# Gated DeltaNet in a hybrid encoder trunk: decays read back as running sums, row groups taken in turn, products with the zero state left out

## The chip, the cores and the metric

The kernel runs on one core of a Trainium2 chip. The metric is the device time of one execution in microseconds (us). A core has TensorE (PE; its weight loads are listed apart as PEld), VectorE (DVE), ScalarE (ACT), GpSimd (POOL) and SyncE (SP), whose queue issues all DMA transfers of this kernel. Each engine works through its own instructions in the order in which they were written into its queue; semaphores hold an instruction back until what it reads is there and what it overwrites has been read. Two memories matter: SBUF, 128 partitions wide, and PSUM, into which TensorE writes.

## What is computed

One layer with three token mixers over 2048 positions, each on its own columns of one input projection:

```python
h = rmsnorm(x, norm_w[l])
u = jnp.einsum('bsd,de->bse', h, w_in[l])
(a_q, a_k, a_v, a_z, g_q, g_k, g_v, g_z, g_b, g_a, r_x, r_z) = jnp.split(u, SPLIT_POINTS, axis=-1)
y_a = diff_attention(a_q, a_k, a_v, ...) * jax.nn.silu(a_z)
y_g = gated_deltanet(g_q, g_k, g_v, g_b, g_a, g_z, ...)
y_r = rg_lru(r_x, ...) * jax.nn.silu(r_z)
x = x + jnp.einsum('bse,ed->bsd', concat(y_a, y_g, y_r), w_out[l])
return rmsnorm(x, final_norm_w)
```

The change is in the second mixer, the gated delta rule (GDN), with 4 heads of 128 columns. Its core, in chunks:

```python
g = jnp.cumsum(g, axis=-1)                     # log decay, summed inside a chunk
decay = jnp.exp(jnp.where(tri, g[..., :, None] - g[..., None, :], -jnp.inf))
Lmat = jnp.where(strict, einsum('id,jd->ij', k_beta, k) * decay, 0.0)
T = triangular_solve(eye + Lmat, eye, lower=True, unit_diagonal=True)
u = T @ v_beta;   w = T @ (k_beta * jnp.exp(g)[..., None])
a_intra = jnp.where(tri, einsum('id,jd->ij', q, k) * decay, 0.0)

def step(state, xs):                           # over the chunks; the first state is zero
    v_new = u_i - w_i @ state
    o = (q_i * exp(g_i)) @ state + a_i @ v_new
    state = state * exp(g_last) + (k_i * exp(g_last - g_i)).T @ v_new
    return state, o
```

## The kernel before

Positions are taken in two halves of 1024 (`hf`), each half in two blocks of 512 (`sb`). The first stage, up to about 1140 us, runs the input projections: a job is 128 columns of `w_in`, and `unit` (L294) makes 128 x 512 outputs of it in 24 products, three for each of 8 slices of the inner dimension, since every f32 operand is split into a high and a low part (L298 to L300). Results go to one of two PSUM buffers `pj`. Everything else of this stage runs as Python generators in `bgs`: after every second slice `unit` calls `pump`, which lets each generator write its next few instructions. So the work of the mixers is laid in small pieces between the projections. The tile framework's scheduler then fixes the order on each engine; the order of the program is its preference, and it moves instructions that would wait. The second stage runs attention and the output projection, and the change does not touch it but for the number of buffers of one tile (`sd`).

The delta rule uses chunks of 128 positions, eight to a half (`NC_H`). In each half `gb_post` (L386) makes the gates once for all heads: `g`, its split in `ghi` and `glo`, and by two small products the running sums and totals, whose exponentials are `gam` and `gl`. For each of four heads, `Gdn.main` (L489) then does the following.

1. Decays, for two groups of four chunks (L517 to L535). With `tri_le` the triangle of ones, GpSimd multiplies it by the chunk's `ghi` and by its `glo` (L522), 8 instructions a group. TensorE multiplies a strict triangle `tri_gt` with both (L528, L531), which gives all differences of running sums in one PSUM tile, and ScalarE takes the exponential into `dec` (L535).
2. Gram products of keys with keys and queries, 4 a group (L543), scaled by `dec` on VectorE (L549) into `la`; the 32x32 diagonal blocks go to DRAM (`ls`, L563) and come back in another layout (`lt`, L573).
3. The inverse. VectorE solves the 32x32 blocks (L590, L596); they pass through DRAM (`ts`) into `pi`, and are transposed into `xi` (L613). Then the blocks are joined on TensorE: a 32-row stage (L626, L635, L639, each product on one 32-row group of the array, for 8 chunks and two pairs of blocks) and a 64-row stage (L650, L658). The products on f32 data run as two passes each, so L626 is 16 products and 32 passes a head.
4. The chunks in turn (L671 to L706): L674 is the key product with the state, L683 the inverse applied to its difference to the values, L685 the query product with the state, L692 the update of the state, L693 the product inside the chunk. ScalarE evacuates twice (L689, L698), and VectorE does the rest.

SP issues the transfers of all this in one order, together with the fetches of weights (`wx`, L117), which run two jobs ahead.

## Time and profile before

| what | value |
|---|---|
| timed runs | 1777.53, 1775.45, 1775.56 us (median 1775.56) |
| profiled execution | 1779.44 us, span 1777.7 us |
| busy share of the span | PE 97%, PEld 81%, DVE 73%, ACT 56%, POOL 20% |
| granted TensorE clock, mean | 0.995 |

A busy share counts the time in which an engine had at least one instruction in work. Products overlap in TensorE, so a share near 100% alone does not say how much work there is: that is read from the starts of successive products. Lines of the profile are those of the kernel before; x2 behind a small product counts its passes. What an engine waited for is inferred from semaphores. Nothing of the second stage is read below, except that both stages share the same TensorE.

### The profile page before, as it was taken

How to read it: one execution, taken by the hardware profiler on the slowest of the kernel's cores; microseconds unless marked ns; L12 is line 12 of the kernel's file. 1: busy time of each engine (PE TensorE's matmuls, PEld its weight loads, DVE VectorE, ACT ScalarE, POOL GpSimd, SP SyncE). 2: the span in 40 equal slices, each digit the busy share in tenths (PEclk: the TensorE clock that was granted, in tenths of full speed). 3: DMA queues.
4: the chain of work that ended last, by engine and by line, in shares of the span. 5: the costliest groups of instructions: out<-in, count | busy, mean ns of one | idle time of the engine just before them, and what ended most of it. 6: DMA issues, size and time to landing. Idle time of an engine off the chain costs nothing.

```text
span 1777.7 us, 28350 instructions
## 1 busy us (share of the span) xinstructions
PE 1721.5 (97%) x9674; PEld 1433.7 (81%) x9674; DVE 1304.3 (73%) x3064; ACT 987.4 (56%) x2500; POOL 363.3 (20%) x591
## 2 busy tenths in 40 slices
PE   7999999999999999999999999989999999999998
PEld 6877878888878887787787888877888888887786
DVE  6566786686776566688678668568777877778896
ACT  6524534435434553352552543458878878877685
POOL 3211401301301122151151140011213213221011
PEclk9999999999999999999999999999999999999999
DMA  6123142241244423424535424597797797596442
GB/s 186 49 80 90 52 117 73 75 109 58 86 125 137 143 72 119 134 87 160 153 100 166 137 86 123 169 259 217 194 244 220 257 247 213 166 277 212 159 143 101
DMA packets 306901, 257.45 MB, mean 145 GB/s; under 512 B 66794, under 2 KB 242116, under 8 KB 306756
## 3 DMA queue, kind: packets, MB, share of 16 engines
q1 hardware_dynamic: 306756, 255.64, 49.6%
q8 instruction: 76, 1.25, 0.3%
q14 instruction: 69, 0.57, 0.1%
HBM read 171.69 MB, written 83.89 MB: 144 GB/s over the span
## 4 chain that ended last, share of the span: by engine, by line
PE 48%; DVE 11%; issue 5%; DMA 4%; POOL 3%; ACT 3%; SPq 0%; DVEq 0%; POOLq 0%; ACTq 0%
PE pj L298 6%; PE pj L299 6%; PE pj L300 6%; PE pj L885 4%; PE pj L883 4%; PE pj L884 4%; PE s L1026 3%; PE s L1027 2%; PE pt L1101 2%; DVE tt L596 1%; PE av L1119 1%; DVE tt L590 1%; PE av L1120 1%; DVE s L363 1%; PE av L1118 1%
## 5 line engine op out<-in xcount | busy, mean ns | idle before, releaser
L298 PE MATMUL pj<-hp,wx 128*128 128x512 f32 x1120 | 463.6, 414 | 2.7 <-DVE sz L375 1.2
L300 PE MATMUL pj<-hp,wx 128*128 128x512 f32 x1120 | 444.3, 397 | 0.0
L299 PE MATMUL pj<-hp,wx 128*128 128x512 f32 x1120 | 443.0, 396 | 0.0
L300 PEld LDWEIGHTS pj<-hp,wx 128*128 128x128 f32 x1120 | 210.6, 188 | 49.4
L298 PEld LDWEIGHTS pj<-hp,wx 128*128 128x128 f32 x1120 | 211.3, 189 | 45.3 <-DVE sz L375 1.4
L299 PEld LDWEIGHTS pj<-hp,wx 128*128 128x128 f32 x1120 | 211.8, 189 | 41.9
L1030 DVE TENSOR_REDUCE nm<-s 128x1 f32<-128x512 f32 (+3 forms) x320 | 191.7, 605 | 27.4 <-PE s L1027 24.0
L1038 ACT ACTIVATE s<-s,nm 128x512 f32<-128x512 f32 (+3 forms) x272 | 170.6, 629 | 52.6 <-DVE nm L1030 51.2
L363 DVE SCALAR_TENSOR_TENSOR s<-raw,pcol,s 128x512 f32<-128x512 f32 x192 | 144.5, 753 | 37.0 <-POOL s L359 34.5
L1026 PE MATMUL s<-hp 128*128 128x512 f32 (+3 forms) x320 | 124.5, 390 | 6.3 <-DMA hp<-k_sp 3.6
L291 DVE TENSOR_TENSOR wx<-wx 128x1024 fp32r<-128x1024 f32 (+1 forms) x77 | 95.6, 1242 | 44.3 <-ACT wx L287 44.2
L287 ACT ACTIVATE wx<-wx 128x1024 fp32r<-128x1024 f32 (+1 forms) x76 | 80.4, 1058 | 77.7 <-PE pj L299 67.2
L1027 PE MATMUL s<-hp 128*128 128x512 f32 (+3 forms) x320 | 117.8, 368 | 0.0
L1101 PE MATMUL pt<-ident,s 128*128 128x128 f32 x544 | 86.1, 274 | 4.0 <-DVE s L1089 3.9
L354 POOL COPY halo<-raw 128x3 f32<-128x3 f32 x48 | 13.2, 275 | 373.1 <-ACT raw L352 367.2
L883 PE MATMUL pj<-g,wx 128*128 128x512 f32 x208 | 85.4, 411 | 0.1
L590 DVE TENSOR_TENSOR tt<-lt,tt 128x248 f32<-128x248 f32 (+30 forms) x248 | 80.8, 326 | 6.5
L1089 DVE SCALAR_TENSOR_TENSOR s<-s,cf,s 128x512 f32<-128x512 f32 (+2 forms) x112 | 75.1, 702 | 11.1 <-ACT s L1077 6.5
L596 DVE TENSOR_TENSOR tt<-tt 128x248 f32<-128x248 f32 (+30 forms) x248 | 78.2, 315 | 6.4
L885 PE MATMUL pj<-g,wx 128*128 128x512 f32 x208 | 82.3, 396 | 0.0
L884 PE MATMUL pj<-g,wx 128*128 128x512 f32 x208 | 81.9, 394 | 0.0
L317 PE MATMUL pj<-wx,hp 128*128 128x264 f32 (+1 forms) x256 | 76.7, 301 | 2.9 <-ACT wx L287 0.9
(341 smaller groups left out, 3958.1 us busy)
## 6 DMA issues: line engine op xcount, KB each, us to landing
wx<-in_w_in_dram SPq DMA_DIRECT2D x78, 512.0 KB, 4.4
wx<-y_sp SPq DMA_DIRECT2D x64, 512.0 KB, 5.8
hp<-k_sp SPq DMA_DIRECT2D x64, 256.0 KB, 6.2
wo_sp<-s SPq DMA_DIRECT2D x48, 256.0 KB, 2.0
v_sp<-s SPq DMA_DIRECT2D x64, 128.0 KB, 2.9
q_sp<-s SPq DMA_DIRECT2D x32, 256.0 KB, 3.2
k_sp<-s SPq DMA_DIRECT2D x32, 256.0 KB, 2.6
y_sp<-go SPq DMA_DIRECT2D x32, 256.0 KB, 2.1
```

Source lines behind the costliest of these rows:

```text
L298: nc.tensor.matmul(ps, wh[:, kt, :], hb[kt][:, 0, :], start=(kt == 0), stop=False)
L299: nc.tensor.matmul(ps, wh[:, kt, :], hb[kt][:, 1, :], start=False, stop=False)
L300: nc.tensor.matmul(ps, wl[:, kt, :], hb[kt][:, 0, :], start=False, stop=(kt == KT - 1))
L363: nc.vector.scalar_tensor_tensor(y, raw[:, t : t + SB], pc(wcol(t)), y, op0=ALU.mult, op1=ALU.add)
L883: nc.tensor.matmul(ps, yh, wh, start=first, stop=False)
L884: nc.tensor.matmul(ps, yh, wl, start=False, stop=False)
L885: nc.tensor.matmul(ps, yl, wh, start=False, stop=last)
L1026: nc.tensor.matmul(ps[:, :n], qq, kh[:, :n], start=True, stop=False)
L1027: nc.tensor.matmul(ps[:, :n], qq, kl[:, :n], start=False, stop=True)
L1030: nc.vector.tensor_reduce(nm[:, u, m, kb : kb + 1], ps[:, :n], axis=AX.X, op=ALU.max, negate=True)
L1038: nc.scalar.activation(ee[:, :n], ps[:, :n], AF.Exp, bias=nm[:, u, m, kb : kb + 1], accum_out=zp[:, u, m, kb : kb + 1],)
L1101: nc.tensor.transpose(pt[:, off + (u - us[0]) * P : off + (u - us[0] + 1) * P], e[(u, kt // 4)][:, (kt % 4) * P : (kt % 4 + 1) * P], ident,)
```

## The change

It has four parts, all in the delta rule.

- Decays. `tri_gt`, `ghi` and `glo`, their GpSimd products and the two TensorE products a group go. Instead `gb_post` makes a third small product, the running sums with chunks in rows, writes them to DRAM (`cs`), and keeps the sums by position in `cum`. Each group reads its four rows of `cs` back, broadcast to all 128 partitions (256 KB in SBUF). ScalarE then takes ReLU(`cum` - value) by chunk, and the exponential of the negative. The reads and the exponentials stand at the start of `main`, before the wait for the keys, and `sd` has two buffers instead of one.
- Row groups. The products of the first two steps of the 32-row stage loop over chunks outside and pairs inside, so successive products are on different row groups.
- The transposed block. The third product of this stage (L639) and its VectorE operation become a 32x32 transpose of the second's result.
- State. For the first chunk of the first half the products with the zero state are left out, and the state is copied instead of updated; for the last chunk of the second half the update is left out.

```diff
@@ -148,12 +148,6 @@
     nc.gpsimd.affine_select(
         tri_le, ones32, pattern=[[1, P]], compare_op=ALU.is_ge, fill=0.0, base=0, channel_multiplier=-1
     )
-    tri_gt = ctile([P, P], "tri_gt", F32R)
-    tri_gt32 = at([P, P], "s16", 16)
-    nc.gpsimd.affine_select(
-        tri_gt32, ones32, pattern=[[-1, P]], compare_op=ALU.is_gt, fill=0.0, base=0, channel_multiplier=1
-    )
-    nc.vector.tensor_copy(tri_gt, tri_gt32)
 
     pcol = ctile([P, N_COLS], "pcol")
     nps = psum.tile([P, SB], F32, name="pps", tag="tp", bufs=3)
...
@@ -401,10 +393,6 @@
         g = at([P, 4, NC_H], "g", 2)
         nc.vector.scalar_tensor_tensor(g, xa, 0.0, ax, op0=ALU.max, op1=ALU.add)
         nc.vector.tensor_tensor(g, g, nea.unsqueeze(2).to_broadcast([P, 4, NC_H]), op=ALU.mult)
-        ghi = at([P, 4, NC_H], "ghi", 2, F32R)
-        nc.vector.tensor_copy(ghi, g)
-        glo = at([P, 4, NC_H], "glo", 2, F32R)
-        nc.vector.tensor_tensor(glo, g, ghi.bitcast(F32), op=ALU.subtract)
         yield
         yield
         yield
@@ -412,13 +400,21 @@
         gf = g.rearrange("p a b -> p (a b)")
         nc.tensor.matmul(pg[:, 0:32], tri_le, gf, start=True, stop=True)
         nc.tensor.matmul(pg[:, 32:64], ones, gf, start=True, stop=True)
+        nc.tensor.matmul(pg[0:32, 64 : 64 + P], gf, tri_le, start=True, stop=True)
...
+
+        cum = at([P, 4, NC_H], "cum", 1)
+        nc.scalar.activation(cum, pg[:, 0:32].rearrange("p (b c) -> p b c", b=4), AF.Copy)
+        cr = at([32, P], "s16", 16)
+        nc.scalar.activation(cr, pg[0:32, 64 : 64 + P], AF.Copy)
+        cs = dram.tile([4 * NC_H, P], F32, name="cs", tag="cs", bufs=2)
+        nc.sync.dma_start(cs, cr)
         ngam = at([P, 4, NC_H], "ngam", 2)
         nc.vector.tensor_scalar_mul(ngam, gam[:, 0], -1.0)
-        r.beta, r.ghi, r.glo, r.gam, r.gl, r.ngam = beta, ghi, glo, gam[:, 0], gam[:, 1], ngam
+        r.beta, r.cum, r.cs, r.gam, r.gl, r.ngam = beta, cum, cs, gam[:, 0], gam[:, 1], ngam
         r.ready = True
 
 
@@ -488,7 +484,26 @@
 
         def main(v):
             h, gbs = v.h, v.gbs
-            while v.nt < 4 or not gbs.ready:
+            while not gbs.ready:
+                yield
+            decs = [at([P, 4, P], "sd", 2) for _ in range(2)]
+            for sb in range(2):
+                r0 = h * NC_H + sb * 4
+                nc.sync.dma_start(
+                    decs[sb].rearrange("p c e -> p (c e)"),
+                    gbs.cs[r0 : r0 + 4].rearrange("r e -> (r e)").unsqueeze(0).to_broadcast([P, SB]),
+                )
+            yield from wait(4)
+            for sb in range(2):
+                for c in range(4):
+                    ci = sb * 4 + c
+                    nc.scalar.activation(
+                        decs[sb][:, c, :], decs[sb][:, c, :], AF.Relu, scale=-1.0,
+                        bias=gbs.cum[:, h, ci : ci + 1],
+                    )
+                nc.scalar.activation(decs[sb], decs[sb], AF.Exp, scale=-1.0)
+                yield
+            while v.nt < 4:
                 yield
             ss = v.ss
             nc.vector.tensor_scalar_add(ss, ss, 4e-6)
@@ -514,25 +529,9 @@
                 kq = v.kq[sb]
                 la = at([P, 4, 2, P], "g5", 5)
                 las.append(la)
-                gmh = at([P, 4, P], "s16", 16, F32R)
-                gml = at([P, 4, P], "s16", 16, F32R)
-                for c in range(4):
-                    ci = sb * 4 + c
-                    for gm, gg in ((gmh, gbs.ghi), (gml, gbs.glo)):
-                        nc.gpsimd.tensor_scalar(
-                            gm[:, c, :], tri_le, gg.bitcast(F32)[:, h, ci : ci + 1], 0.0,
-                            op0=ALU.mult, op1=ALU.add,
-                        )
+
+                dec = decs[sb]
                 yield from wait(3)
-                pe = tp()
-                nc.tensor.matmul(
-                    pe, tri_gt, gmh.rearrange("p c e -> p (c e)"), start=True, stop=False
-                )
-                nc.tensor.matmul(
-                    pe, tri_gt, gml.rearrange("p c e -> p (c e)"), start=False, stop=True
-                )
-                dec = at([P, 4, P], "sd", 1)
-                nc.scalar.activation(dec, pe.rearrange("p (c e) -> p c e", c=4), AF.Exp)
                 nc.vector.tensor_tensor(
                     cd[:, sb * 4 : sb * 4 + 4], cc[:, sb * 4 : sb * 4 + 4], dec[:, :, P - 1],
                     op=ALU.mult,
@@ -621,8 +620,8 @@
             ]
             zs32 = at([P, NC_H, 32], "zs", 1)
             pz = tp().rearrange("p (c e) -> p c e", c=NC_H)
-            for a, b in pairs:
-                for c in range(NC_H):
+            for c in range(NC_H):
+                for a, b in pairs:
                     nc.tensor.matmul(
                         pz[b, c, 0:32], lt_ab(c, a, b), xi[a, c, a], start=True, stop=True
                     )
@@ -630,19 +629,15 @@
                 nc.vector.tensor_copy(zs32[b], pz[b, :, 0:32])
             yield
             pu = tp().rearrange("p (c e) -> p c e", c=NC_H)
-            for a, b in pairs:
-                for c in range(NC_H):
+            for c in range(NC_H):
+                for a, b in pairs:
                     nc.tensor.matmul(
                         pu[a, c, 0:32], zs32[b, c, :], pi[b, c, b], start=True, stop=True
                     )
-            for c in range(NC_H):
-                nc.tensor.matmul(
-                    pu[32:64, c, 0:32], pi[32:64, c, 32:64], zs32[32:64, c, :],
-                    start=True, stop=True,
-                )
-            nc.vector.tensor_scalar_mul(xi[32:64, :, 0:32], pu[32:64, :, 0:32], -1.0)
             for a, b in pairs:
                 nc.vector.tensor_scalar_mul(pi[a, :, b], pu[a, :, 0:32], -1.0)
+
+            nc.vector.transpose(xi[32:64, :, 0:32], pi[0:32, :, 32:64])
             yield
             lo, up = slice(0, 64), slice(64, 128)
             pz = tp().rearrange("p (c e) -> p c e", c=NC_H)
@@ -670,36 +665,51 @@
                 so = at([P, 4], "so", 2)
                 for c in range(4):
                     ci = sb * 4 + c
-                    pks = psum.tile([P, P], F32, name="ch", tag="ch", bufs=2)
-                    nc.tensor.matmul(pks, v.kq[sb][:, c, 0, :], S_, start=True, stop=True)
+
+                    none, final = v.hf == 0 and ci == 0, v.hf == 1 and ci == NC_H - 1
                     ct = at([P, 4, P], "ct", 2)
-                    br = ct[:, 0, :]
-                    nc.vector.scalar_tensor_tensor(
-                        br, pks, gbs.ngam[:, h, ci : ci + 1], v.vb[sb][:, c, :],
-                        op0=ALU.mult, op1=ALU.add,
-                    )
-                    yield
+                    br = v.vb[sb][:, c, :]
+                    if not none:
...
+                        yield
                     py = psum.tile([P, P], F32, name="ch", tag="ch", bufs=2)
                     nc.tensor.matmul(py, pi[:, ci, :], br, start=True, stop=True)
                     po = psum.tile([P, 2, P], F32, name="oq", tag="oq", bufs=1)
-                    nc.tensor.matmul(po[:, 0, :], v.kq[sb][:, c, 1, :], S_, start=True, stop=True)
-                    yd = ct[:, 1, :]
-                    nc.vector.tensor_scalar(yd, py, cd[:, ci : ci + 1], None, op0=ALU.mult)
+                    if not none:
+                        nc.tensor.matmul(
+                            po[:, 0, :], v.kq[sb][:, c, 1, :], S_, start=True, stop=True
+                        )
+                    if not final:
+                        yd = ct[:, 1, :]
+                        nc.vector.tensor_scalar(yd, py, cd[:, ci : ci + 1], None, op0=ALU.mult)
                     y = ct[:, 2, :]
                     nc.scalar.activation(y, py, AF.Copy)
                     yield
-                    pst = psum.tile([P, P], F32, name="ch", tag="ch", bufs=2)
-                    nc.tensor.matmul(pst, v.kp[sb][:, c, :], yd, start=True, stop=True)
+                    if not final:
+                        pst = psum.tile([P, P], F32, name="ch", tag="ch", bufs=2)
+                        nc.tensor.matmul(pst, v.kp[sb][:, c, :], yd, start=True, stop=True)
                     nc.tensor.matmul(po[:, 1, :], las[sb][:, c, 1, :], y, start=True, stop=True)
-                    nc.vector.scalar_tensor_tensor(
-                        S_, S_, gbs.gl[:, h, ci : ci + 1], pst, op0=ALU.mult, op1=ALU.add
-                    )
-                    ay = ct[:, 3, :]
-                    nc.scalar.activation(ay, po[:, 1, :], AF.Copy)
-                    nc.vector.scalar_tensor_tensor(
-                        os_[:, c, :], po[:, 0, :], gbs.gam[:, h, ci : ci + 1], ay,
-                        op0=ALU.mult, op1=ALU.add,
-                    )
+                    if none:
+                        nc.vector.tensor_copy(S_, pst)
+                    elif not final:
+                        nc.vector.scalar_tensor_tensor(
+                            S_, S_, gbs.gl[:, h, ci : ci + 1], pst, op0=ALU.mult, op1=ALU.add
+                        )
+                    if none:
+                        nc.scalar.activation(os_[:, c, :], po[:, 1, :], AF.Copy)
+                    else:
+                        ay = ct[:, 3, :]
+                        nc.scalar.activation(ay, po[:, 1, :], AF.Copy)
+                        nc.vector.scalar_tensor_tensor(
+                            os_[:, c, :], po[:, 0, :], gbs.gam[:, h, ci : ci + 1], ay,
+                            op0=ALU.mult, op1=ALU.add,
+                        )
                     jk = at([P, SB], "junk", 1, BF16)
                     nc.scalar.activation(
                         jk[:, :P], os_[:, c, :], AF.Square, accum_out=so[:, c : c + 1]
@@ -913,7 +923,7 @@
-                pe = at([P, SB], "sd", 1)
+                pe = at([P, SB], "sd", 2)
```

Three places of the order on an engine follow, of the kernel before and of the changed one. Lines of the changed kernel are its own: L290 to L292 are the projection there (L298 to L300 before).

TensorE, first head, first group of decays, before (`s_1013` and `s_1014` are the two operands made by GpSimd):

```order
405 L298 MATMUL pj<-hp,wx 128x512
406 L299 MATMUL pj<-hp,wx 128x512
407 L300 MATMUL pj<-hp,wx 128x512
408 L528 MATMUL tp<-s_1013,tri_gt 128x512 [waits PE_49,Pool_49]
409 L531 MATMUL tp<-s_1014,tri_gt 128x512 [waits Pool_49]
410 L543 MATMUL tp<-g_608 128x256 x2
411 L543 MATMUL tp<-g_608 128x256 [waits Activation_49]
412 L543 MATMUL tp<-g_608 128x256
413 L298 MATMUL pj<-hp,wx 128x512
```

The same place in the changed kernel, where L542 is the Gram product:

```order
406 L290 MATMUL pj<-hp,wx 128x512
407 L291 MATMUL pj<-hp,wx 128x512
408 L292 MATMUL pj<-hp,wx 128x512
409 L542 MATMUL tp<-g_600 128x256 [waits PE_49]
410 L542 MATMUL tp<-g_600 128x256 x3
411 L290 MATMUL pj<-hp,wx 128x512
```

The two triangle products and their waits for GpSimd are gone; the Gram products follow the projection.

ScalarE, second head of the first half, second group, before (L477 evacuates the transposed values, L689 and L698 belong to the chunks of the head before):

```order
184 L371 ACTIVATE s_2245<-pj 128x512 [waits PE_49]
185 L535 ACTIVATE sd<-tp 128x512 [waits DVE_49,PE_49,Activation_49]
186 L689 ACTIVATE ct<-ch 128x128 [waits DVE_49]
187 L698 ACTIVATE ct<-oq 128x128 [waits PE_49]
188 L704 ACTIVATE junk,so<-go 128x128 [waits DVE_49]
189 L477 ACTIVATE s_2321<-tp,nk 128x128 [waits PE_49]
190 L477 ACTIVATE s_2321<-tp,nk 128x128 x3
```

The same place in the changed kernel (L500 is the ReLU, L504 the exponential):

```order
195 L363 ACTIVATE s_2206<-pj 128x512 [waits DMAHW1_49,PE_49]
196 L692 ACTIVATE ct<-ch 128x128 [waits DVE_49]
197 L708 ACTIVATE ct<-oq 128x128 [waits PE_49]
198 L714 ACTIVATE junk,so<-go 128x128 [waits DVE_49]
199 L500 ACTIVATE sd<-sd,cum 128x128 [waits DMAHW5_49]
200 L500 ACTIVATE sd<-sd,cum 128x128 x3
201 L504 ACTIVATE sd<-sd 128x512 [waits Activation_49]
202 L473 ACTIVATE s_2290<-tp,nk 128x128 [waits PE_49]
203 L473 ACTIVATE s_2290<-tp,nk 128x128 x3
204 L279 ACTIVATE wx<-wx 128x1024 [waits DMAHW6_49,PE_49]
205 L363 ACTIVATE s_2302<-pj 128x512 [waits DMAHW3_49,PE_49]
```

The exponential of a PSUM tile is replaced by four ReLUs and an exponential that wait for a transfer (DMAHW5), for the decays of the head after; they stand behind the chunk's evacuations and ahead of the transposed values.

SP at the same head in the changed kernel (before, the same eight writes L563 and then L573 stand without anything between):

```order
98 L562 DMA ls<-g_2081 32x4x32 [waits DMAHW1_49,DVE_49]
99 L562 DMA ls<-g_2081 32x4x32
100 L562 DMA ls<-g_2081 32x4x32 [waits DMAHW3_49]
101 L562 DMA ls<-g_2081 32x4x32
102 L492 DMA sd<-cs 128x512
103 L562 DMA ls<-g_2170 32x4x32 [waits DMAHW6_49,DVE_49]
104 L562 DMA ls<-g_2170 32x4x32 [waits DMAHW7_49]
105 L562 DMA ls<-g_2170 32x4x32 [waits DMAHW0_49]
106 L562 DMA ls<-g_2170 32x4x32 [waits DMAHW1_49]
107 L492 DMA sd<-cs 128x512 [waits DMAHW2_49]
108 L572 DMA lt<-ls 32x1024 [waits DMAHW4_49,DMAHW6_49,DMAHW3_49,DMAHW7_49,DMAHW1_49,DMAHW0_49]
```

Each broadcast read (L492) of the next head stands right behind the writes that follow the last use of the buffer it fills.

## Rows read from the trace of the kernel before

**Rows 1.** The page's busy times, and its chain of waits by line.
```profile
PE 1721.5 (97%) x9674; PEld 1433.7 (81%) x9674; DVE 1304.3 (73%) x3064; ACT 987.4 (56%) x2500; POOL 363.3 (20%) x591
...
PE pj L298 6%; PE pj L299 6%; PE pj L300 6%; PE pj L885 4%; PE pj L883 4%; PE pj L884 4%; PE s L1026 3%; PE s L1027 2%; PE pt L1101 2%; DVE tt L596 1%; PE av L1119 1%; DVE tt L590 1%; PE av L1120 1%; DVE s L363 1%; PE av L1118 1%
```

**Rows 2.** TensorE timeline near 306 us: start, length, line, operands, passes.
```profile
305.32 0.49 PE L683 MATMUL ch<-ct,g 128*128 128x128 f32 x2
...
306.10 0.40 PE L299 MATMUL pj<-hp,wx 128*128 128x512 f32 x1
306.33 0.39 PE L300 MATMUL pj<-hp,wx 128*128 128x512 f32 x1
...
307.24 0.38 PE L692 MATMUL ch<-ct,s 128*128 128x128 f32 x2
307.46 0.48 PE L693 MATMUL oq<-ct,g 128*128 128x128 f32 x2
307.70 0.48 PE L298 MATMUL pj<-hp,wx 128*128 128x512 f32 x1
308.02 0.40 PE L299 MATMUL pj<-hp,wx 128*128 128x512 f32 x1
```

**Rows 3.** Stretches: length, busy PE, PEld, DVE, ACT, POOL, then granted clock, DMA.
```profile
140.00:1140.00 1000.00, 981.59 (x5512) 805.00 (x5511) 718.96 (x1662) 435.55 (x1036) 211.43 (x383) 1.00 0.38 110
```

**Rows 4.** Waits of TensorE: total us, times, longest.
```profile
PE tp L528 <- POOL s L522: 2.7, 4, 1.3
```

**Rows 5.** Line L528 alone, idle before it with weight loads: us, times.
```profile
  POOL s L522: 7.5, 9
```

**Rows 6.** TensorE timeline, 32-row stage of the first head.
```profile
152.57 1.09 PE L626 MATMUL tp<-xi,g 32*32 32x32 f32 x32
153.60 0.50 PE L298 MATMUL pj<-hp,wx 128*128 128x512 f32 x1
...
156.01 0.21 PE L639 MATMUL tp<-zs,g 32*32 32x32 f32 x1
...
156.10 0.19 PE L635 MATMUL tp<-g,zs 32*32 32x32 f32 x1
156.12 0.57 PE L639 MATMUL tp<-zs,g 32*32 32x32 f32 x13
156.62 0.50 PE L298 MATMUL pj<-hp,wx 128*128 128x512 f32 x1
```

**Rows 7.** Groups by line: count, busy us, mean ns, idle before and its releaser.
```profile
L645 DVE TENSOR_SCALAR g<-tp 32x256 f32<-32x256 f32 x16 | 6.7, 417 | 0.5
...
L613 DVE STREAM_TRANSPOSE xi<-g 32x256 f32<-32x256 f32 x24 | 10.4, 433 | 13.2 <-DMA g<-ts 12.7
...
L371 ACT ACTIVATE s<-s 128x512 f32<-128x512 f32 x48 | 30.3, 631 | 63.4 <-DVE s L363 63.1
...
L689 ACT ACTIVATE ct<-ch 128x128 f32<-128x128 f32 x64 | 17.6, 275 | 66.1 <-DVE ct L687 66.1
```

**Rows 8.** ScalarE timeline, second head.
```profile
214.34 0.19 ACT L704 ACTIVATION_READ_ACCUMULATOR junk<-go 128x1 f32 x1
217.10 1.14 ACT L477 ACTIVATE s<-tp,nk 128x128 f32<-128x128 f32 x4 [2.57 <-PE tp L473]
...
219.21 0.58 ACT L371 ACTIVATE s<-pj 128x512 f32<-128x512 f32 x1
```

**Rows 9.** SP timeline, second head.
```profile
211.29 5.33 SPq L563 DMA_DIRECT2D ls<-g  x8
```

**Rows 10.** DMA issues: count, KB each, median us to landing.
```profile
wo_sp<-s SPq DMA_DIRECT2D x48, 256.0 KB, 2.0
...
s<-in_w_out_dram SPq DMA_DIRECT2D x24, 256.0 KB, 4.1
```

**Rows 11.** TensorE timeline, first head of the second half.
```profile
732.82 1.53 PE L635 MATMUL tp<-g,zs 32*32 32x32 f32 x29 [2.75 <-DVE zs L630]
```

**Rows 12.** The stretch around it, columns as in rows 3.
```profile
730.00:735.00 5.00, 2.25 (x49) 2.21 (x48) 2.96 (x5) 0.00 (x0) 0.00 (x0) 0.74 0.74 193
```

More of the change, by code (lines that the diff above doesn't have):

```diff
@@ L174, in tile_trunk @@
     st = [st2[h // 2][:, h % 2, :] for h in range(4)]
-    for h in range(4):
-        nc.gpsimd.memset(st[h], 0.0)
     def tp():
@@ L672, in main @@
                     ci = sb * 4 + c
-                    pks = psum.tile([P, P], F32, name="ch", tag="ch", bufs=2)
-                    nc.tensor.matmul(pks, v.kq[sb][:, c, 0, :], S_, start=True, stop=True)
+                    none, final = v.hf == 0 and ci == 0, v.hf == 1 and ci == NC_H - 1
                     ct = at([P, 4, P], "ct", 2)
-                    br = ct[:, 0, :]
-                    nc.vector.scalar_tensor_tensor(
-                        br, pks, gbs.ngam[:, h, ci : ci + 1], v.vb[sb][:, c, :],
-                        op0=ALU.mult, op1=ALU.add,
-                    )
-                    yield
+                    br = v.vb[sb][:, c, :]
+                    if not none:
+                        pks = psum.tile([P, P], F32, name="ch", tag="ch", bufs=2)
+                        nc.tensor.matmul(pks, v.kq[sb][:, c, 0, :], S_, start=True, stop=True)
+                        br = ct[:, 0, :]
+                        nc.vector.scalar_tensor_tensor(
+                            br, pks, gbs.ngam[:, h, ci : ci + 1], v.vb[sb][:, c, :],
+                            op0=ALU.mult, op1=ALU.add,
+                        )
+                        yield
                     py = psum.tile([P, P], F32, name="ch", tag="ch", bufs=2)
```

3 lines of the change are left out of this document (added).

## Prediction

> **What bounds the kernel now.** I read the page's busy times and its chain first: TensorE is busy 97% of the span, VectorE 73%, ScalarE 56%, GpSimd 20%, and the chain that ended last is mostly TensorE lines, the projections (L298 to L300) ahead of all others [rows 1]. A busy TensorE here contains the pipelined tail of each product, so I looked next at starts in its timeline: in a projection one 512-column product follows the other after 0.23 us (306.10, 306.33), although each is shown 0.39 us long [rows 2]. So a product is worth its start-to-start time, and not its bar. The table by stretches says the same for the stage that the change touches (projections, delta rule and recurrence, up to about 1140 us): TensorE busy 981.6 of 1000 us, ScalarE 435.6 [rows 3]. So in this stage what is taken from TensorE's stream comes off the end, nearly one for one, unless a new wait takes its place.
>
> **The change part by part.**
>
> Decay products. Each of 8 heads (4 per half) has two groups of four chunks, and each group loses two 128x512 products with the triangle, 16 of L528 and 16 of L531. In the order of the changed kernel the projection's last product is followed by the Gram products at once. 32 x 0.23 = 7.4 us off the stream.
>
> Waits for GpSimd. The operands of these products are 8 GpSimd multiplications a group. TensorE's own list has L528 waiting for them 2.7 us, 4 times, 1.3 us the longest [rows 4]; the weight loads that run ahead of it waited 7.5 us, 9 times [rows 5]. These two are my bounds; I take 3.5, near the first, since a weight load may wait while a product still runs (2.7 plus some 0.2 of an emptied pipeline, four times). The GpSimd time itself is spent beside everything else and is worth nothing.
>
> Third product of the 32-row stage. The 16 passes of L639 a head go. In one head L635's last pass starts at 156.10 and the projection resumes at 156.62; after the L626 group it resumes 0.13 us after the last pass (152.57 + 1.09 - 0.19 = 153.47, then 153.60) [rows 6]. So it could resume at 156.23: 0.39 x 8 = 3.1 us. VectorE's L643 (as long as its neighbour L645, 417 ns) is replaced by a 32-row transpose (433 ns, as L613) [rows 7]. The 64-row products now wait for the third VectorE operation instead of the first, about 0.85 us later; by the order 6 or 9 projection products (1.4 to 2.1 us) stand between, which hide it. Without them it would cost 0.85 x 8.
>
> Alternating row groups. L626 and L635 are 32 passes a head each. The 32 of L626 start (1.09 - 0.19)/31 = 29 ns apart on the mean, and the last 13 of L639, all in one row group, (0.57 - 0.19)/12 = 32 ns. Where L639 (rows 32 to 63) meets the end of L635 (rows 96 to 127), passes of the two interleave: the first of L639 starts at 156.01, the last of L635 at 156.10 and the next of L639 at 156.12, seven starts in turn, so 6 steps in 0.11 us, 18 ns each [rows 6]. If the alternation holds that pace, a group of 32 takes 0.58 instead of 0.93 us: 0.35 x 2 x 8 = 5.6 us. Bounds: nothing, and 32/2 = 16 ns a pass, 6.9 us; a loss I exclude, since the change of group there costs no gap. I take 5.
> The Trainium skill speaks against this step. "TensorEngine Tiling (Array Packing)", section Restrictions and Gotchas (Gotcha 1: PSUM Pressure), says that different row tiles write to different PSUM banks and cannot use the same bank at once; all these passes write one PSUM tile of 2 KB a partition. The interleaved starts of L635 and L639, which write that same tile, are against the rule in this trace. By the rule this term would be zero and the sum 5 us smaller.
>
> Zero state and last state. For each of 4 heads the first chunk drops the products with the zero state (L674, L685) and the last chunk the state update (L692). A 128-column f32 product is two passes and takes 0.22 us of the stream (307.24 to 307.46); the return to projections makes its first product 0.32 instead of 0.23 us (307.70 to 308.02) [rows 2]. L674 is a visit of its own: 0.31; the other two 0.22 each. 0.75 x 4 = 3.0 us. The few VectorE and ScalarE operations that go with them were hidden behind TensorE.
>
> What is added on TensorE. One product of 128 columns in each half's gate work: 2 x 0.22 = 0.4. And the new order goes from projections to f32 products 306 times instead of 294 in this stage, at 0.09 a return: 1.1 us.
>
> What is added on ScalarE. Per group four ReLUs of 128x128 with a bias per partition and one exponential of 128x512. The nearest rows are L477, four with a scale per partition in 1.14 us [rows 8], and L371 from SBUF, 631 ns [rows 7]; I take 1.8 us a group, 28 us in all, and one exponential a group (L535) goes. ScalarE has 56% of this stage free [rows 3], so the work itself hides; it would cost at most its 28 us. The order has as many table loads as before.
>
> What is added as transfers, and the new wait. In each half the running sums go to DRAM, and every group is read back as a broadcast of 256 KB. Transfers of 256 KB land 2.0 us after issue (wo_sp, a write) to 4.1 us (rows of w_out, a read) [rows 10]; I take 3. On SP the read stands behind four ls writes of the head before and waits for no buffer that these did not wait for, so SP is held no longer; only in the first head of a half does SP stand until the sums have landed, under 2 us, and behind it is a weight fetch two jobs ahead of its use. On ScalarE the first ReLU is parked until its data land, and everything queued there is parked too. Second head: the eight ls writes run from 211.29 to 216.62 [rows 9], so the read, after four of them, goes out at about 213.5 and lands at 215.5 to 217.6; ScalarE gets there at 214.5 and is through 1.8 us after the landing, at 217.3 to 219.4. Next in its queue are the four L477 (here at 217.10), a weight split and the evacuation of a projection (219.21) [rows 8]. All of it comes up to 2.3 us late; a projection has a second PSUM buffer and takes 24 x 0.23 = 5.5 us to fill it, so TensorE does not feel it there. It can where a state product of the head before waits for ScalarE: from L683 to L693 there are 307.46 - 305.32 = 2.14 us [rows 2], less 0.22 for the product and 0.28 for the evacuation L689 [rows 7], 1.6 of slack. 14 groups are exposed. Bounds: 0, and a parked ScalarE (4.1 + 1.8) less that slack at each, 4.3 x 14 = 60. I take 2, close to the lower end, since the queue of the second head has the chunk's evacuations ahead of the ReLU.
>
> Sum: -7.4 - 3.5 - 3.1 - 5.0 - 3.0 + 0.4 + 1.1 + 2.0 = -18.5 us. The profiled execution took 1779.44 us (span 1777.7 and 1.7 around it), so it would be 1760.9. The median of the timed runs, 1775.56, lies 3.9 lower; there it is 1757.1, say 1757.
>
> One thing I leave as it is: TensorE waits 2.75 us for VectorE before 732.82 [rows 11], and in the same 5 us the granted clock falls, 0.74 on the mean, so partly 1.2 instead of 2.4 GHz [rows 12]. VectorE's order is the same there, so I keep both. If they went, or came a second time, some 6 us would go or come.
>
> **Rivals.**
> One bank, no overlap: passes of alternating groups wait for each other's writes. The interleaving in rows 6 speaks against it; for it, that the interleaving is seven passes long and no row shows 32. 1757 + 5 = 1762.
> Waits come back: TensorE no longer stands for GpSimd, but ScalarE holds state products and transposed chunks, and the 3.5 us plus some 8 more return (8 of 14 groups at 1 us). 1757 + 11.5, about 1768.
> No change: the gain is swallowed whole, as it would be if the chain of one head and not the stream set the pace. Against it stand 981.6 busy of 1000 us. 1774.
> Slower, ScalarE parked on the broadcast: the reads land 4.1 us after issue and 6 of the 14 groups catch a state product, 4.3 x 6 = 26 us for the 2 that I took: 1757 + 24 = 1781. It decides when a group costs TensorE (18.5 + 2)/14 = 1.5 us on the mean. For it: ScalarE works strictly in its order, and in the second head the ReLU does come before its data. Against it: the evacuations at that place have 1.6 us and more to spare.
>
> **How the numbers follow.** Forecast 0.52; one bank 0.20; waits come back 0.13; no change 0.07; slower 0.08. The range runs from 1750 (the alternation at 6.9, the waits for GpSimd at 7.5, ScalarE's 2 at nothing: 1757 - 7.9) to 1769, which takes in the second and third case and leaves out the last two. Own range of the likeliest: 1750 to 1762. A change under 0.2%, 3.6 us, can't be told from none here; so faster 0.85, same 0.07, slower 0.08.
>
> **What would show it.** In the profile after: the Gram products start 0.23 us after a projection product, with no wait on GpSimd; a group of 32 passes in the 32-row stage is about 0.75 us long with its tail (right) or still about 1.0 (one bank); the projection resumes 0.13 us after the second group; ScalarE's ReLUs wait 0 to 3 us for the broadcast, and TensorE hardly for ScalarE. The prediction is wrong if TensorE's list of waits gets entries on ScalarE above some 5 us, or if its stream in the stage gets shorter and the stage does not.

## The result, and the profile after

The changed kernel took 1757.87 us in the median of the first runs (four, 1750.52 to 1758.26) against 1775.51, ratio 0.9881 [0.9860, 0.9901]. On two later occasions it took 1753.75 and 1754.69, with ratios 0.9864 [0.9845, 0.9882] and 0.9855 [0.9838, 0.9872]. The forecast time was right. The gain in the first runs was 17.6 us; at an equal clock (below) it is 24.4, larger than the forecast sum of 18.5.

**One clock for all runs.** Every run lists its mean granted clock. It moves between 0.989 and 0.999, and inside one kernel 0.001 of it goes with 1.31 us (141 runs of all kernels here, compared within each). "At full clock" below is a run's time less 1.31 us for each 0.001 that its clock lacks to 1; the error is a 95% interval from the scatter of the runs, rather too narrow where there are only four to six. On the four later occasions the kernel before came to 1771.1 to 1772.2 us at full clock, so its runs are taken together.

| kernel | runs | median us | mean clock | at full clock | against before |
|---|---|---|---|---|---|
| before (later occasions) | 55 | 1779.42 | 0.9940 | 1771.4 ± 0.3 | |
| changed | 13 | 1754.74 | 0.9938 | 1747.0 ± 0.5 | -24.4 |
| before + row groups | 12 | 1775.69 | 0.9928 | 1765.7 ± 0.7 | -5.7 |
| before + transposed block | 12 | 1776.03 | 0.9938 | 1767.6 ± 0.9 | -3.8 |
| before + decays | 6 | 1768.35 | 0.9928 | 1759.5 ± 1.3 | -11.9 |
| before + state | 6 | 1789.86 | 0.9902 | 1776.7 ± 0.7 | +5.3 |
| before, GpSimd's operands gone | 12 | 1774.13 | 0.9926 | 1764.8 ± 0.7 | -6.6 |
| the same + state | 6 | 1770.70 | 0.9923 | 1760.6 ± 1.2 | -10.8 |
| changed, old row-group order | 6 | 1760.40 | 0.9935 | 1751.9 ± 0.8 | -19.5 |
| changed, reads issued late | 4 | 1755.85 | 0.9938 | 1747.4 ± 1.1 | -24.0 |
| changed, second group later | 4 | 1760.38 | 0.9948 | 1754.1 ± 0.9 | -17.3 |
| changed, later in one head | 5 | 1752.21 | 0.9954 | 1745.5 ± 0.9 | -25.9 |

The page of the changed kernel, busy times, to be held against [rows 1]:

```profile
PE 1697.3 (97%) x9494; PEld 1414.3 (81%) x9494; DVE 1286.4 (74%) x3043; ACT 1005.7 (58%) x2568; POOL 305.3 (17%) x458
```

TensorE is busy 24.2 us less, and its share of the span is the same. The stretches (length, then busy TensorE, weight loads, VectorE, ScalarE, GpSimd, then granted clock, DMA) say where the time went; the first answers to [rows 3], the second is attention and output:

```profile
140.00:1114.00 974.00, 958.42 (x5336) 785.18 (x5335) 704.08 (x1647) 449.40 (x1085) 160.47 (x271) 1.00 0.39 116
1114.00:1748.00 634.00, 610.68 (x3499) 521.61 (x3497) 494.90 (x1168) 479.75 (x1291) 117.97 (x138) 0.99 0.72 210
```

Near the end of the first stage the same state product stands 26.5 us earlier (before, then changed), of 28.9 us between the two spans:

```profile
1150.53 0.39 PE L692 MATMUL ch<-ct,s 128*128 128x128 f32 x2
1124.06 0.38 PE L696 MATMUL ch<-ct,s 128*128 128x128 f32 x2
```

Some 3.4 of the 26.5 us is clock: the stretch at 1.2 GHz behind [rows 11], 6.8 us long in the trace, is missing in this execution of the changed kernel.

The TensorE timeline of the 32-row stage in the first head, and of the Gram products of a later group; the first answers to [rows 6]:

```profile
151.78 0.69 PE L625 MATMUL tp<-xi,g 32*32 32x32 f32 x32
152.41 0.50 PE L290 MATMUL pj<-hp,wx 128*128 128x512 f32 x1
...
154.00 0.69 PE L634 MATMUL tp<-g,zs 32*32 32x32 f32 x32
154.63 0.50 PE L290 MATMUL pj<-hp,wx 128*128 128x512 f32 x1
...
209.45 0.39 PE L292 MATMUL pj<-hp,wx 128*128 128x512 f32 x1
209.68 1.89 PE L542 MATMUL tp<-g 128*128 128x256 f32 x8
```

A group of 32 passes is 0.69 us long instead of 1.09: (0.69 - 0.19)/31 = 16 ns a pass on the mean. The single starts in the trace come 7 and 25 ns apart in turn, 32 ns from one to the next but one. That is the distance that the prediction read from L639 within one row group, so the two row groups seem to run beside each other, each at its own pace. The projection resumes 0.63 us after the start of the group, 0.13 after its last pass (0.69 - 0.19 = 0.50). The Gram products start 0.23 us behind a projection product. All three signs came as forecast.

The waits of TensorE from 140 to 1140 us (total, times, longest), the top ones and two lower ones on ScalarE; below them two entries of ScalarE's list for the whole execution:

```profile
PE pj L290 <- DVE s L367: 2.4, 2, 1.4
PE tp L634 <- DVE zs L629: 2.2, 1, 2.2
PE ch L682 <- DVE ct L676: 2.2, 6, 0.8
PE pj L309 <- ACT wx L279: 1.9, 1, 1.9
...
PE pj L309 <- ACT gb L329: 1.2, 2, 0.6
...
PE oq L697 <- ACT ct L692: 0.4, 2, 0.3
...
ACT sd L500 <- DMA sd<-cs: 16.6, 7, 6.5
ACT sd L500 <- DVE go L739: 3.7, 1, 3.7
```

No entry on GpSimd's decay operands is left. ScalarE does stand for the broadcast, up to 6.5 us at a time, longer than the 0 to 3 us that I looked for. All of TensorE's entries on ScalarE in this stage come to 3.5 us, under the 5 us that I named as a sign of being wrong; they are taken up below. ScalarE's new work by line:

```profile
L500 ACT ACTIVATE sd<-sd,cum 128x128 f32<-128x128 f32 x64 | 20.6, 394 | 23.8 <-DMA sd<-cs 16.6 <-DVE go L739 3.7 <-DVE g L548 3.4
L504 ACT ACTIVATE sd<-sd 128x512 f32<-128x512 f32 x16 | 10.0, 628 | 0.3
...
sd<-cs SPq DMA_DIRECT2D x16, 256.0 KB, 3.4
```

A group costs (20.6 + 10.0)/16 = 1.9 us (estimate 1.8), and the read lands after 3.4 us (taken: 3).

### The profile page after: what moved, and what is told of

The parts are those of the page before. It is cut to its first block, busy times and chain, and to the rows that moved or that the text cites. A ratio compares the mean times of both kernels' runs of the same rounds, so it can differ in the third digit from the quotient of the medians.

```text
span 1748.8 us, 27889 instructions
## 1 busy us (share of the span) xinstructions
PE 1697.3 (97%) x9494; PEld 1414.3 (81%) x9494; DVE 1286.4 (74%) x3043; ACT 1005.7 (58%) x2568; POOL 305.3 (17%) x458
## 4 chain that ended last, share of the span: by engine, by line
PE 61%; DVE 10%; issue 7%; DMA 4%; ACT 3%; POOL 2%; SPq 1%; POOLq 0%; DVEq 0%; ACTq 0%
PE pj L290 10%; PE pj L291 10%; PE pj L292 10%; PE pj L895 3%; PE pj L893 3%; PE pj L894 3%; PE s L1036 2%; PE s L1037 2%; PE pt L1111 2%; DVE s L355 2%; DVE tt L589 1%; DVE tt L595 1%; DMA wx<-xo_sp 1%; PE tp L542 1%; PE av L1130 1%
## 5 line engine op out<-in xcount | busy, mean ns | idle before, releaser
L290 PE MATMUL pj<-hp,wx 128*128 128x512 f32 x1120 | 461.4, 412 | 2.4 <-DVE s L367 2.4
L292 PE MATMUL pj<-hp,wx 128*128 128x512 f32 x1120 | 444.5, 397 | 0.0
L292 PEld LDWEIGHTS pj<-hp,wx 128*128 128x128 f32 x1120 | 210.5, 188 | 47.9
L290 PEld LDWEIGHTS pj<-hp,wx 128*128 128x128 f32 x1120 | 211.0, 188 | 45.3 <-DVE s L367 2.9
```

What stands on the lines that cost most here:

```text
L290: nc.tensor.matmul(ps, wh[:, kt, :], hb[kt][:, 0, :], start=(kt == 0), stop=False)
L292: nc.tensor.matmul(ps, wl[:, kt, :], hb[kt][:, 0, :], start=False, stop=(kt == KT - 1))
```

## Experiments

**The changed kernel again**, twice, unchanged.

> The changed kernel once more, on another occasion. Its profiled execution took 1750.5 us and its three timed runs 1757.9, with mean granted clocks of 0.996 and 0.991 to 0.993. Theory A (clock): the runs fall into two groups about 7 us apart, and the longer ones have a mean clock lower by 0.003 to 0.005, that is two more stretches of some 6.8 us at 1.2 GHz somewhere in the projections; the median is again 1757 to 1758.5. Theory B (the short execution is the rule and something else disturbed the others): the median is 1750 to 1752. Theory C (the long ones are the rule and the clock has no part in it): all runs at 1757 to 1758 with a clock of 0.996.

> The changed kernel a third time, as the yardstick for the two runs beside it. All theories: 1753 to 1758, by a mean granted clock of 0.991 to 0.995; with 1.45 us for each 0.001 of clock (the slope over the repeated runs of the kernel before) it comes to 1745 to 1747 at full clock.

1753.75 and 1754.69 us, mean clock 0.994 each, 1747.0 at full clock like the first occasion's. So A in kind: time follows the clock (1750.5 us at 0.996, 1758 at 0.991 to 0.993), but not in two groups; the predicted median was 3 us too long for these occasions.

**Each part alone on the kernel before.** Where an expected time of these runs counts from the 1775.5 us of the first occasion, read it as a difference; the kernel before ran at 1779 beside them. Row groups:

```diff
-            for a, b in pairs:
-                for c in range(NC_H):
+            for c in range(NC_H):
+                for a, b in pairs:
```

> The kernel before with the alternating row groups alone (the loops of the first two steps of the 32-row stage swapped). Theory A (passes on two row groups start twice as often): the groups of 32 passes shrink from about 1.03 to 0.68 us, 16 groups, 5 to 6 us in all: 1770. Rival (one bank, passes wait for each other): groups stay at 1.03 us, 1775.5. Second rival (the gain of the whole change is larger than its sum because the shorter groups also spare the clock its dips): below 1766, with the half-clock stretch near 735 us gone.

1775.69 us, ratio 0.9980 [0.9969, 0.9991]; -5.7 at full clock. The clock was 0.0012 lower than that of before, which takes back 1.6 us, so the raw difference alone, 3.7 us, lay between A and the rival. A holds, by the length of the groups too; the second rival falls, since the clock did not rise. Its counterpart, the changed kernel with the old order:

> The changed kernel with the old loop order in the 32-row stage (pairs outside, chunks inside). Theory A (the parts add): the 5 to 6 us that the alternation gave to the kernel before are lost here too, 1759 to 1760 where the changed kernel has 1753.8, and a group of 32 passes is 1.03 us long again. Rival (the parts overlap, the freed time is eaten by waits in the full kernel): under 2 us lost, 1754 to 1756.

1760.40 us, 0.9897 [0.9881, 0.9914]; 4.9 lost at full clock. The first head's passes there:

```profile
152.26 1.09 PE L625 MATMUL tp<-xi,g 32*32 32x32 f32 x32
153.28 0.50 PE L290 MATMUL pj<-hp,wx 128*128 128x512 f32 x1
```

The group is back at 1.09 us. Both ways the order is worth some 5 us.

The transposed block (third product and its VectorE operation out, the transpose in):

```diff
-                nc.tensor.matmul(pu[32:64, c, 0:32], pi[32:64, c, 32:64], zs32[32:64, c, :], ...)
-            nc.vector.tensor_scalar_mul(xi[32:64, :, 0:32], pu[32:64, :, 0:32], -1.0)
+            nc.vector.transpose(xi[32:64, :, 0:32], pi[0:32, :, 32:64])
```

> The kernel before with the third product of the 32-row stage replaced by the transpose alone. Theory A (the passes' starts are their price): 8 x 0.39 to 0.45 = 3.1 to 3.6 us less at an equal granted clock, 1775 to 1776 where the kernel before has 1779. Rival (the later third VectorE operation makes the 64-row products wait): up to 0.85 x 8 = 6.8 us more, so +3: 1782, with entries of L650's successor on VectorE in TensorE's waits.

1776.03 us, 0.9984 [0.9972, 0.9996]; -3.8 at full clock. A; no wait on VectorE for the 64-row products appeared among TensorE's larger waits.

The decays alone (the change's hunks in `gb_post` and `main`, `tri_gt` and `sd`):

> The kernel before with the decays by broadcast read, ReLU and exponential alone (sd with two buffers), everything else as before. Theory A (the prediction's terms: -7.4 for 32 products, -2.7 to -7.5 for waits for GpSimd, +0.4, about +1, +2 for ScalarE): 1767 to 1771, middle 1768.5. Theory B (the change's surplus over its sum, 8 us or so, comes from GpSimd's work that is gone): 1759 to 1764. Theory C (ScalarE parked costs as much as the products were worth): 1774 to 1777.

1768.35 us, 0.9947 [0.9928, 0.9966]; -11.9 ± 1.3 at full clock. As a difference A had -5 to -9 and B -12 to -17, so it is at the edge of B. What lies behind that is priced by the next kernel, with the products kept and GpSimd's multiplications gone (the exponential also gets the scale -1, not shown):

```diff
-                    for gm, gg in ((gmh, gbs.ghi), (gml, gbs.glo)):
-                        nc.gpsimd.tensor_scalar(gm[:, c, :], tri_le, ...)
+                one4 = onesr.unsqueeze(1).to_broadcast([P, 4, P])
...
-                    pe, tri_gt, gmh.rearrange("p c e -> p (c e)"), start=True, stop=False
+                    pe.rearrange("p (c e) -> p c e", c=4), tri_gt, one4, start=True, stop=False
```

> The kernel before with its two decay products a group and their exponential kept, but with a constant tile of ones as their operand, so that GpSimd's eight multiplications a group go (the decays are then not those of the reference). This prices the waits for GpSimd alone. Theory A (the waits shown at L528): 2 to 3 us less at an equal clock, 1776 to 1777. Theory B (the 7.5 us shown ahead of the weight loads): 1771 to 1772. Theory C (GpSimd slows VectorE or other engines as well, so that its 93 us of work are worth more): below 1769.

1774.13 us, 0.9976 [0.9964, 0.9988]; -6.6 ± 0.8 at full clock, near B. TensorE's timeline shows why its list of waits [rows 4] told too little. The kernel before, then the one with the constant tile at the same place:

```profile
922.65 0.40 PE L300 MATMUL pj<-hp,wx 128*128 128x512 f32 x1
924.36 0.47 PE L528 MATMUL tp<-s,tri_gt 128*128 128x512 f32 x1 [1.31 <-POOL s L522]
924.67 0.40 PE L531 MATMUL tp<-s,tri_gt 128*128 128x512 f32 x1
925.14 1.97 PE L543 MATMUL tp<-g 128*128 128x256 f32 x8
```

```profile
920.31 0.40 PE L300 MATMUL pj<-hp,wx 128*128 128x512 f32 x1
920.87 0.47 PE L520 MATMUL tp<-ones,tri_gt 128*128 128x512 f32 x1 [0.16 <-DVE g L541]
921.18 0.40 PE L523 MATMUL tp<-ones,tri_gt 128*128 128x512 f32 x1
921.65 1.97 PE L535 MATMUL tp<-g 128*128 128x256 f32 x8
```

From start to start L300 to L528 is 1.71 us, 1.48 over the usual 0.23, and the list counts 1.31: a wait starts there only where the bar of the product before ends, 0.17 us late, and shorter waits don't show at all. L531 and L543 come 0.31 and 0.47 us later instead of 0.23, but so they do with the constant tile; what went at this place is 1.15 us at L528. Summed over the 16 groups of the profiled execution, the starts from the product ahead to the Gram products add up to 16.8 us in the kernel before and to 11.6 with the constant tile. Of the 6.6, that is 5.2; where the rest comes from is not shown.

The state alone (the change's hunks in the recurrence, and the clearing of the state):

> The kernel before without the products of the zero state and without the last update alone. Theory A (products are worth their start-to-start time): 4 x 0.75 = 3 us less, 1772.5. Rival B (the first chunk's chain of products and evacuations was on the path as well, since each step of it waits for VectorE): up to 2 us a head, 1767 to 1769. Rival C (hidden anyway): 1775.5.

1789.86 us, 1.0062 [1.0043, 1.0081]; +5.3 at full clock: none of the three. TensorE's longest list entry from 140 to 1140 us, then GpSimd's timeline of one group, VectorE's scaling of the Gram products that GpSimd waits to mask, and TensorE at the same place:

```profile
PE tp L526 <- POOL s L520: 10.3, 5, 3.5
```

```profile
337.18 0.37 POOL L520 TENSOR_SCALAR s<-tri_le,ghi 128x128 fp32r<-128x128 f32 x1
341.18 0.97 POOL L555 TENSOR_SCALAR_AFFINE_SELECT g<-g 128x512 f32<-128x512 f32 x1 [3.63 <-PE pj L298]
342.14 0.37 POOL L520 TENSOR_SCALAR s<-tri_le,glo 128x128 fp32r<-128x128 f32 x1
```

```profile
340.19 0.86 DVE L547 SCALAR_TENSOR_TENSOR g<-tp,cc,sd 128x256 f32<-128x256 f32 x2
```

```profile
341.96 0.40 PE L298 MATMUL pj<-hp,wx 128*128 128x512 f32 x1
344.29 0.50 PE L526 MATMUL tp<-s,tri_gt 128*128 128x512 f32 x1 [1.93 <-POOL s L520]
```

With the shorter recurrence the scheduler put the masking of the first group's Gram products (L555) in front of seven of the second group's eight multiplications (L520). GpSimd stood 3.63 us for it, and TensorE then for GpSimd. (The profile names a projection product as what ended GpSimd's wait; by the code L555 masks what L547 writes, and that ended at 341.05, 0.13 us before.) Whether the edit itself cost anything is told by making it where GpSimd has no such work:

> The kernel before without the zero-state products and last update, and with the decay products fed from a constant tile as in the run beside this one (decays not those of the reference). The state edit alone came out 5 us slower at an equal clock (1789.9, clock 0.990, against 1779.1 at 0.994), and its TensorE waited 10.3 us for GpSimd at L526 where the kernel before waits 2.0. Theory A (the edit itself is worth its 3 us or so, and the loss is GpSimd's queue alone): with GpSimd's operands gone it is 3 to 4 us faster than the run with the constant tile and the old state products. Rival B (the edit itself costs, by the shorter chain of the first chunks meeting VectorE and ScalarE sooner): 0 to 5 us slower than that run.

1770.70 us, 0.9955 [0.9940, 0.9970]; at full clock 4.2 ± 1.4 faster than the run with the constant tile alone. A. The edit also moves waits. In the kernel before, in the seventh chunk of the first half's last head, TensorE stands for the state's update:

```profile
567.26 0.28 PE L319 MATMUL pj<-wx,hp 128*128 128x256 f32 x1
569.82 0.49 PE L674 MATMUL ch<-st,g 128*128 128x128 f32 x2 [2.28 <-DVE st L694]
```

In the changed kernel the chain of this head begins one product earlier, and the same chunk's product follows at once:

```profile
557.97 0.28 PE L311 MATMUL pj<-wx,hp 128*128 128x256 f32 x1
558.09 0.39 PE L674 MATMUL ch<-st,g 128*128 128x128 f32 x2
```

With the constant tile, TensorE's entries on the state fall likewise, and new short ones of the same chain come (the first row without the state edit, the others with it; 140 to 1140 us):

```profile
PE ch L666 <- DVE st L686: 3.4, 3, 2.3
...
PE ch L677 <- DVE ct L671: 1.6, 6, 0.4
PE ch L691 <- DVE ct L685: 0.9, 2, 0.6
PE ch L669 <- DVE st L696: 0.5, 1, 0.5
```

What goes and what comes nearly cancel, so the 4.2 ± 1.4 is not more than the products' 3.0 by anything that these lists show.

**The reads issued later.** The reads are issued behind the four slots instead of ahead of them.

```diff
+            yield from wait(4)
             for sb in range(2):
                 r0 = h * NC_H + sb * 4
                 nc.sync.dma_start(
...
                 )
-            yield from wait(4)
```

> The changed kernel with the broadcast reads issued where the ReLUs are written, four slots later, so that ScalarE is parked for the whole landing of 3.4 us or more in every group of reads. This prices the step in which a parked ScalarE holds back TensorE. Theory A (the projections' second PSUM buffer and the slack of the state products cover it): ScalarE's waits for the reads grow from 16.6 us to 25 to 40 us in all, and the time stays within 2 us. Theory B (the price of the prediction's slower case, 4.3 us at each group that catches a state product): 4 to 8 groups, 17 to 34 us slower, with entries on ScalarE in TensorE's waits.

1755.85 us beside 1754.69, 0.4 ± 1.2 at full clock. But the edit did not park ScalarE longer. Its idle time ahead of the ReLUs, the number behind the last bar, is 24.5 us here, then 24.2 in an unchanged repetition of the changed kernel, and was 23.8 in that kernel's first profile:

```profile
L500 ACT ACTIVATE sd<-sd,cum 128x128 f32<-128x128 f32 x64 | 20.6, 394 | 24.5 <-DMA sd<-cs 24.3
L500 ACT ACTIVATE sd<-sd,cum 128x128 f32<-128x128 f32 x64 | 20.7, 394 | 24.2 <-DMA sd<-cs 24.2
```

Against the 16.6 us that the expected text starts from, only the name of what came last changed, from VectorE to the transfer. So this run prices nothing, neither A's cover nor B. What can be read is the trace of the changed kernel: ScalarE stands ahead of the ReLUs near 101, 213, 218, 340, 348, 662, 667, 783 and 908 us, and TensorE's entries on ScalarE (3.5 us from 140 to 1140 us) lie at 303, 428, 584, 589 and 604 us, none beside such a place. The kernel before has 1.5 us of them and the kernel with the decays alone 0.9. So no wait of TensorE is seen behind a parked ScalarE.

**A pause and the clock.** In the changed kernel TensorE waits before L634 in the first head of the second half, as the kernel before does [rows 11]. Rows of one of its later executions, then a stretch behind it, with the granted clock, 0.68, after the five busy columns:

```profile
720.75 0.40 PE L292 MATMUL pj<-hp,wx 128*128 128x512 f32 x1
723.49 0.95 PE L634 MATMUL tp<-g,zs 32*32 32x32 f32 x32 [2.35 <-DVE zs L629]
...
725.44 0.63 PE L290 MATMUL pj<-hp,wx 128*128 128x512 f32 x1
725.87 0.63 PE L291 MATMUL pj<-hp,wx 128*128 128x512 f32 x1
```

```profile
725.00:730.00 5.00, 5.00 (x27) 3.66 (x25) 1.65 (x4) 1.88 (x2) 1.24 (x4) 0.68 0.62 117
```

The two projection products start 0.43 us apart instead of 0.23, at 1.2 GHz. To take the pause away, the second group of passes was put two slots later, first in every head, then in this one alone:

```diff
                 nc.vector.tensor_copy(zs32[b], pz[b, :, 0:32])
-            yield
+            yield from wait(3)
```

```diff
                 nc.vector.tensor_copy(zs32[b], pz[b, :, 0:32])
-            yield
+            yield from wait(3 if v.hf == 1 and h == 0 else 1)
```

> The changed kernel with the second group of passes of the 32-row stage placed three slots instead of one behind the copies that it reads. In the first head of the second half TensorE waits 2.2 us there for VectorE, and a stretch at 1.2 GHz follows in several executions. Theory A (the wait goes, and with it part of the dips): 2.2 us less at full clock, 1743 to 1744, and no half-clock stretch between 715 and 745 us; in time 1748 to 1752. Rival B (the wait only changes its place, since VectorE is behind for longer than two slots or the next reader waits in its stead): same time within 1 us. Rival C (every head's chain ends two slots later and the state products of the next head meet other work): 2 to 6 us slower.

> The changed kernel with the second group of the 32-row stage placed three slots behind its copies in the first head of the second half alone; all other heads keep one slot. The run with three slots in every head lost the pause and every half-clock stretch of the projections in its profile (mean clock 0.9948 over the runs), but came out 7 us slower at full clock, by state products that met other work. Theory A (the pause and the dip can be had by this one head): the 2.2 us pause goes, no half-clock stretch between 715 and 745 us, 2 to 3 us less at full clock, and in time 1749 to 1752 where the changed kernel has 1754.7 beside the same kernel before. Rival B (one head moved costs a seventh or so of the 7 us and its pauses come back at the state products): 1753 to 1756. Rival C (the pause is not what lowers the clock): the pause goes and the stretch at 1.2 GHz near 725 us is still there.

In every head: 1760.38 us, 0.9891 [0.9874, 0.9908]; the pause and the dip are gone, and it is 7.2 ± 1.0 us slower at full clock: C's sign, above its 2 to 6 us. The loss is spread over many small waits at transposes and state products; which of them are cause and which follow was not settled. In one head: 1752.21 us, 0.9840 [0.9818, 0.9861], beside the changed kernel's 0.9855 [0.9838, 0.9872]. The clock in its profile stays up:

```profile
725.00:730.00 5.00, 4.87 (x44) 3.72 (x43) 2.15 (x5) 1.15 (x2) 1.73 (x3) 1.00 0.53 108
```

It is the fastest here, by 2.5 us in the medians and 1.5 ± 1.1 at full clock, though the ratios overlap and five runs don't make that clear of noise. It is A's sign at less than A's size: the new order waits elsewhere (L682 for VectorE 3.1 us instead of 2.2). Of the twelve profiled executions that have the pause, nine have a stretch at 1.2 GHz within some 10 us of it; of the two without it, none. That the pause brings the stretch on is likely by this, not shown: three pauses had no stretch.

## Why the prediction was right, point by point

- **What bounds the kernel.** Right: TensorE's stream in the first stage. The stage's 1000 us became 974, and 26.5 of the 28.9 us between the two profiled executions were gained by its end.
- **Decay products and GpSimd.** The waits for GpSimd are the mis-sized term. I gave the waits 3.5 us, near the lower of two bounds, "since a weight load may wait while a product still runs". Measured: 6.6 ± 0.8, near the 7.5 of the weight loads [rows 5]. The rest of the decay edit, products less additions, comes to -11.9 + 6.6 = -5.3 ± 1.4; by my terms -7.4 + 0.4 + 2.0 and half of the 1.1 for added visits, about -4.5. The visits were not measured apart.
- **ScalarE parked, +2.0.** ScalarE was parked, 23.8 us in all, and no wait of TensorE is seen behind it. By time the term is open: the rest of the decay edit leaves 1.2 ± 1.4 us for it (-5.3 + 7.4 - 0.4 - 0.5), so neither 0 nor 2 is excluded, and the late reads did not test the cover that I named. The slower rival, 24 us more, did not come.
- **Third product, -3.1.** Measured -3.8 ± 0.9. The later third VectorE operation hid, as worked out.
- **Alternating row groups, -5.0.** Measured -5.7 ± 0.8 on the kernel before and 4.9 ± 1.0 in the changed one; the pass came every 16 ns on the mean, the upper bound's pace. The 29 ns that I read for the old order is 32 in one row group with an overlap where the groups change. The one-bank rival fell. The Trainium skill, "TensorEngine Tiling (Array Packing)", section Restrictions and Gotchas (Gotcha 1: PSUM Pressure), says that different row tiles cannot access the same PSUM bank at once. By the 0.69 us of a group this does not hold for these passes, which all write one tile of 2 KB a partition. They write different partitions of it (32 to 63 and 96 to 127 in the first step, 0 to 31 and 64 to 95 in the second); no run here has alternating passes that write the same ones.
- **Zero and last state, -3.0.** -4.2 ± 1.4 where GpSimd's operands are gone, +5.3 where they are not. My term was a sum of products, and 3.0 lies inside the first. The order that the scheduler makes around the products had no term: with GpSimd's operands in place it cost the difference, 9.5 ± 1.6 us. In the changed kernel they are gone, so the omission did no harm there.
- **The sum.** Parts apart: -5.7 - 3.8 - 11.9 - 4.2 = -25.6 ± 2.3, the whole -24.4 ± 0.6, so the parts add if the state is taken with the decays. The prediction had -18.5. Of the 6 us between, 3.1 are GpSimd's waits. The rest is in pieces of about 1 us (row groups, transposed block, state, the rest of the decays), each within its error.
- **Why the time still came out right.** That 1757.87 lies beside 1757 is luck, since the gain was 6 us larger than the sum. "If they went, or came a second time, some 6 us would go or come": on the first occasion the clock was 0.991 to 0.993 in the three timed runs, worth 9 to 12 us against full clock. Before's clocks of that occasion are not listed but for the profiled execution, 0.995; by the 1.31 us for 0.001, 1775.5 us would go with some 0.997. So about 6 us of gain were covered by the clock. That is inferred, not shown, and it need not have been that one stretch: the three timed runs left no trace.

## What to carry to other kernels

Price a wait on a pipelined engine by the distance between starts, not by the wait list, which counts only from the end of the last bar; here the time landed near the bound from the weight loads that run ahead. Before a run that is to hold an engine up longer is read, look whether the engine's idle time grew in all, not whether one releaser's entry did. An edit that only removes work can lose time where it lets a scheduler reorder an in-order queue that another engine waits for, so test it together with the edit that takes that queue out. Compare runs at one granted clock when gains are below one per cent: here 0.001 of it was worth 1.3 us, a third of the smaller parts of this change.

## What was not expected of the hardware

Passes on alternating 32-row groups ran at 16 ns each on the mean over a whole group of 32, half of the 32 ns in one row group. A pause of TensorE of 2 to 3 us was followed by a stretch at 1.2 GHz in nine of twelve executions and not in three, with the same instructions: the same kernel's profiled execution had none there at 1750.5 us, and its next one had.
